# Low halves of the split gate and up weights: a subtraction on VectorE, or an adding transfer issued by GpSimd

## The chip, the cores and the metric

The kernel runs on one core of one Trainium2 chip. The metric is the device time of one execution in microseconds (us). Before the change the median of three executions is 1720.19 us (1717.99 to 1720.61). Trace times below count from the start of the span of one profiled execution, which itself took 1718.67 us.

## What is computed

One decoder layer on 576 tokens (512 of a prompt, 64 of eight short sequences) with model width 1024. It has three parts: a gated feed-forward block, a token mixer, and a second gated feed-forward block. The change touches the two feed-forward blocks:

```
def swiglu(h, w_gate, w_up, w_down):
    return (jax.nn.silu(h @ w_gate) * (h @ w_up)) @ w_down

h = modulate(rms_norm(x, n1_g), sh1, sc1)
x = x + 0.5 * g1 * swiglu(h, w1_gate, w1_up, w1_down)
```

`w_gate` and `w_up` are 1024 x 2816 in float32, `w_down` is 2816 x 1024. Everything is float32.

## The kernel before, in words

**High and low halves.** TensorE multiplies in a rounded format (float32r). To keep float32 accuracy every operand is split in two: `hi` is the rounded copy, `lo` is the source minus `hi`. A product is then three matmuls: hi x hi, hi x lo, lo x hi (`prod`, lines 675 to 683: for each of four chunks `wh*xh`, `wh*xl`, `wl*xh`, so 12 matmuls of 128x288 and the third of them is the first that reads the weight's `lo`). The split of a weight tile is made by `put_hi` (line 692, ScalarE writes `hi`) and `put_lo` (line 700, VectorE subtracts, line 707).

**Pairs.** The hidden width is cut into 22 blocks of 128 columns. Blocks 0 and 1 are computed plainly (`Plain`); each block from 2 on is a `Pair`: its gate and up columns are taken together as a 2x2 block product with seven products instead of eight (`p1` to `p7`). The weights of a pair come as two raw tiles `p` and `q` (float32, 128x1024 each, in `wraw`). From them four split tiles are made, each holding `hi` and `lo`, in the buffer ring `whl`:

- a: blocks a11 and a22, from `p` (128x1024), read by products p1 and p4
- b: block a12, from half of `q` (128x512), read by p2
- s: sums s3 and s1, from the tile `sum` that step `S` writes (line 818), read by p5 and p7
- u: sums s2 and s4, from the same tile `sum` after the steps `U` and `V` have overwritten its two halves (lines 829 and 832), read by p6 and p3

There is one tile `sum`, and in the feed-forward blocks the ring `whl` has four buffers. A buffer is free once the last product that reads it has ended.

**Order of the work.** For pair i the function `ffn` (line 928) emits: the splits of pair i (`splits`, line 840), p1(i), p2(i), the end of the pair before, p4(i-1), then p5(i), p6(i), p3(i), p7(i). After blocks 4, 10, 15 and 21 (`GROUPS`) the down projection of the group follows, 16 rows of matmuls at line 522; in the first three of these it stands between p6 and p3. A scheduler turns this into one fixed order per engine; it uses its own estimate of durations and may move instructions of one engine past each other where their data allow. On the chip each engine then runs its list strictly in order.

Pair 2 of each block is split step by step in a hand-written order (`BEGIN`, `INTO_FFN2`) by `put_hi` and `put_lo`; pairs 3 to 21 go through `splits`. So `splits` runs 19 times per feed-forward block, 38 times in all. The end of a pair on VectorE and ScalarE: line 892 multiplies p4's result in, lines 720 and 723 split the gated result.

GpSimd has little to do in these blocks: line 509, one small add for each down projection row. All loads are issued by SyncE (SP): raw weights at line 713, down weights at line 130.

Of the kernel before, what the change touches and what calls it, by code (L numbers as in the profile page):

```python
# [10 lines left out]
AF = mybir.ActivationFunctionType  # L11
ALU = mybir.AluOpType
# [63 lines left out]
def layer_kernel(ctx: ExitStack, tc: tile.TileContext, a):  # L76
    nc = tc.nc
    PE, DVE, ACT, POOL = nc.tensor, nc.vector, nc.scalar, nc.gpsimd
# [36 lines left out]
    def weight(tag, shape, dt, bufs):  # L115
        turn[tag] += 1
        own = now[tag] is not None and turn[tag] % (bufs + 1) == 0
        return (now[tag] if own else wp).tile(
            [P] + shape, dt, tag=tag, name=nm(tag), bufs=1 if own else bufs
        )  # L120
# [4 lines left out]
    def whl(shape):  # L125
        return weight("whl", shape, F32R, 4)
# [121 lines left out]
    for i in range(2):  # L248
        for n in range(NT):
            rows = P if n < 4 else NS  # L250
            t = first.tile([rows, 512], F32, name=nm("xt"))
            src = a["x_prompt"][0, n * P:(n + 1) * P] if n < 4 else a["x_sample"].rearrange("b l d -> (b l) d")
# [436 lines left out]
        return t  # L689

    class Weights:
        def put_hi(self, names, src, neg=False):
            hl = whl([2, len(names), 512])
            if neg:
                ACT.activation(out=hl[:, 0], in_=src, func=AF.Copy, scale=-1.0)
            else:
                ACT.copy(out=hl[:, 0], in_=src)  # L697
            self.hl[names] = hl, src, neg
# [96 lines left out]
    class Pair(Weights):  # L795
# [42 lines left out]
            self.put_lo(("s2", "s4"))  # L838

        def splits(self):  # L840
            for f in (self.ah, self.al, self.bh, self.bl, self.S, self.Sh, self.Sl, self.U, self.V, self.Uh, self.Ul):
                f()

        def p1(self):
            self.A = bank()
# [141 lines left out]
    for i in range(2):  # L987
        for n in range(NT):
            m = P if n < 4 else NS
            ACT.activation(  # L990
                out=junk[0:m, i], in_=xtok[n, i], func=AF.Square, accum_out=ss[0:m, i, n:n + 1]
# [54 lines left out]
    for c in range(KC):  # L1046
# [5 lines left out]
        out=t5, in0=r5, scalar=-0.5 / D, in1=r5, op0=ALU.mult, op1=ALU.mult)  # L1052
    steps["r51"] = lambda: DVE.scalar_tensor_tensor(
        out=t5, in0=s5, scalar=D * EPS, in1=t5, op0=ALU.add, op1=ALU.mult)
# [3 lines left out]
        out=xall[:, :, NP:T], in_=psS[:, 0:KC * NS].rearrange("p (c t) -> p c t", c=KC))  # L1058
# [432 lines left out]
    for n in range(NT):  # L1491
        m = P if n < 4 else NS
# [7 lines left out]
        out=rs.bitcast(I32), in0=t5.bitcast(I32), scalar1=-1.0, scalar2=float(0x5F3759DF), op0=ALU.mult, op1=ALU.add  # L1500
# [7 lines left out]
    for g in range(8):  # L1508
        DVE.tensor_tensor(
            out=wd8[:, g, :].rearrange("p (b l) -> p b l", l=LS),  # L1510
# [326 lines left out]
```

## Time and profile before

| what | value |
|---|---|
| median of 3 executions | 1720.19 us |
| the profiled execution, its own time | 1718.67 us |
| its span (first to last instruction) | 1716.6 us |
| TensorE (PE) busy | 1683.7 us, 98% |
| VectorE (DVE) busy | 1049.4 us, 61% |
| ScalarE (ACT) busy | 686.6 us, 40% |
| GpSimd (POOL) busy | 209.0 us, 12% |
| first feed-forward block's matmuls | about 36 to 452 us |
| second feed-forward block's matmuls | about 1310 to 1707 us |

How to read the rows that follow: in a timeline row stand the start, the duration, the engine, the line of the kernel, the operation, the tiles (output <- input), the count, and in brackets how long the engine had stood idle and what ended that. `whl<-sum` is a split of an s or u tile, `whl<-wraw` of an a or b tile; `xs` and `xa` are the split activations. PE is the matmul, PEld the weight load, SPq a transfer issued by SyncE. A `PE ... x12` row is one product. In the table of waits a row reads: engine and line that waited, `<-` what it waited for, total us, how often, the longest. In a table of windows, `PEclk` is the granted TensorE clock as a share of full speed.

### The profile page before, as it was taken

The page shows a single profiled execution, that of the slowest core. Times are in us where ns is not written, and L with a number is a line of the kernel's source. Part 1 is how long each engine was busy: PE and PEld are TensorE (multiplying, and loading weights), DVE is VectorE, ACT ScalarE, POOL GpSimd, SP SyncE. Part 2 cuts the span into 40 slices and gives each one's busy share as a digit, 9 for nine tenths or more (in the row PEclk, how much of TensorE's full clock was granted, in tenths as well). Part 3 has the DMA queues.
Part 4 walks back from the last instruction along what each step waited for, and adds up shares of the span by engine and source line. Part 5 has one row for each costly group of instructions (what it writes and reads, how often), then busy time and mean ns, then how long its engine had stood idle before and what let it go on. Part 6 is the DMA issues. An engine that isn't in the chain of part 4 may idle for free.

```text
span 1716.6 us, 30444 instructions
## 1 busy us (share of the span) xinstructions
PE 1683.7 (98%) x12588; PEld 1610.9 (94%) x12588; DVE 1049.4 (61%) x1758; ACT 686.6 (40%) x1137; POOL 209.0 (12%) x263
## 2 busy tenths in 40 slices
PE   7999999999999999999999999999999999999997
PEld 4879999999999999999999889999999999999997
DVE  6856847676765745745745546422547958666773
ACT  5533524335534333333333333322235525344354
POOL 0000000000421302302202101220021000000002
PEclk9999999999999999999999999999999999999999
DMA  9443444323454433444424335342330323323231
GB/s 301 132 145 98 134 139 129 99 87 95 146 163 140 142 115 125 132 123 125 149 83 143 100 115 161 103 154 75 99 103 21 87 80 92 99 84 89 86 99 56
DMA packets 279773, 199.52 MB, mean 116 GB/s; under 512 B 9801, under 2 KB 253769, under 8 KB 279634
## 3 DMA queue, kind: packets, MB, share of 16 engines
q1 hardware_dynamic: 279634, 197.58, 38.4%
q8 instruction: 98, 1.61, 0.4%
q14 instruction: 41, 0.34, 0.1%
HBM read 183.12 MB, written 14.42 MB: 115 GB/s over the span
## 4 chain that ended last, share of the span: by engine, by line
PE 88%; DVE 4%; DMA 4%; ACT 2%; issue 1%; SPq 0%; POOL 0%; POOLq 0%; DVEq 0%; ACTq 0%
PE ps L522 47%; PE ps L679 24%; PE ps L1236 5%; PE ps L1452 3%; PE ps L265 2%; DMA wraw<-in_w_down_dram 1%; DMA ada<-in_w_ada_dram 1%; DVE whl L707 1%; PE ps L1366 1%; PE ps L1244 1%; PE ps L1328 1%; DMA xa<-in_w_ada_dram 1%; ACT whl L697 1%; PE ps L1372 1%; PE ps L1344 0%
## 5 line engine op out<-in xcount | busy, mean ns | idle before, releaser
L522 PE MATMUL ps<-xa,whl 128*128 128x288 f32 x2784 | 378.4, 295 | 0.5 <-DVE whl L142 0.3
L522 PEld LDWEIGHTS ps<-xa,whl 128*128 128x128 f32 x2784 | 370.9, 188 | 7.6 <-issue 3.4
L679 PE MATMUL ps<-xa,whl 128*128 128x288 f32 x2064 | 292.8, 296 | 1.9 <-ACT whl L697 1.0
L679 PEld LDWEIGHTS ps<-xa,whl 128*128 128x128 f32 x2064 | 279.1, 188 | 10.5 <-issue 2.5
L142 DVE TENSOR_TENSOR whl<-wraw,whl 128x1024 fp32r<-128x1024 f32 x100 | 126.2, 1270 | 212.4 <-ACT whl L141 208.4
L522 PE MATMUL ps<-c,wd 128*128 128x288 f32 x1824 | 246.7, 295 | 0.0
L522 PEld LDWEIGHTS ps<-c,wd 128*128 128x128 f32 x1824 | 243.2, 188 | 2.6 <-issue 1.7
L679 PE MATMUL ps<-xs,whl 128*128 128x288 f32 x1680 | 239.7, 296 | 1.6 <-ACT sn L688 1.4
L679 PEld LDWEIGHTS ps<-xs,whl 128*128 128x128 f32 x1680 | 228.5, 188 | 7.5 <-ACT sn L688 4.9
L522 PE MATMUL ps<-c,whl 128*128 128x288 f32 x1368 | 194.9, 298 | 0.0
L522 PEld LDWEIGHTS ps<-c,whl 128*128 128x128 f32 x1368 | 184.1, 188 | 2.7 <-DVE S L1391 0.8
L141 ACT CAST whl<-wraw 128x1024 fp32r<-128x1024 f32 x100 | 104.0, 1046 | 107.3 <-PE ps L522 47.6
L509 POOL TENSOR_TENSOR x<-x,s 128x64 f32<-128x64 f32 x72 | 34.4, 478 | 909.4 <-DVE s L508 909.2
L503 DVE SCALAR_TENSOR_TENSOR x<-ps,gate,x 128x288 f32<-128x288 f32 (+1 forms) x128 | 61.5, 483 | 135.3 <-PE ps L522 134.9
L697 ACT CAST whl<-sum 128x1024 fp32r<-128x1024 f32 x80 | 84.0, 1050 | 86.3 <-DVE sum L832 58.2
L707 DVE TENSOR_TENSOR whl<-sum,whl 128x1024 fp32r<-128x1024 f32 x80 | 98.0, 1225 | 30.2 <-ACT whl L697 28.2
L697 ACT CAST whl<-wraw 128x1024 fp32r<-128x1024 f32 (+1 forms) x84 | 70.6, 841 | 98.5 <-PE ps L679 84.8
L1236 PEld LDWEIGHTS ps<-whl,xa 128*128 128x128 f32 x768 | 94.1, 194 | 5.1 <-DVE whl L142 3.4
L1236 PE MATMUL ps<-whl,xa 128*128 128x256 f32 x768 | 95.6, 286 | 3.2 <-DVE whl L142 3.2
L909 ACT CAST wd<-wraw 128x640 fp32r<-128x640 f32 (+2 forms) x58 | 45.3, 782 | 123.6 <-PE ps L522 116.7
L707 DVE TENSOR_TENSOR whl<-wraw,whl 128x1024 fp32r<-128x1024 f32 (+1 forms) x84 | 81.2, 967 | 9.5 <-ACT whl L697 9.1
L688 ACT COPY sn<-ps 128x288 f32<-128x288 f32 x126 | 50.1, 398 | 59.2 <-PE ps L679 57.7
(264 smaller groups left out, 1835.2 us busy)
## 6 DMA issues: line engine op xcount, KB each, us to landing
wraw<-in_w_in_dram SPq DMA_DIRECT2D x80, 512.0 KB
ada<-in_w_ada_dram SPq DMA_DIRECT2D x56, 512.0 KB
wraw<-in_w_gate_dram SPq DMA_DIRECT2D x88, 256.0 KB
wraw<-in_w_up_dram SPq DMA_DIRECT2D x88, 256.0 KB
wraw<-in_w_down_dram SPq DMA_DIRECT2D x32, 384.0 KB
wraw<-in_w_down_dram SPq DMA_DIRECT2D x32, 320.0 KB
S<-in_state_ret_dram SPq DMA_DIRECT2D x32, 256.0 KB
wraw<-in_w_b_dram SPq DMA_DIRECT2D x16, 512.0 KB
```

The source lines that it names most:

```text
L141: ACT.copy(out=hi, in_=raw)
L142: (eng or DVE).tensor_tensor(out=lo, in0=raw, in1=hi.bitcast(F32), op=ALU.subtract)
L503: DVE.scalar_tensor_tensor(out=x[:, o:o + w], in0=ps[:, :w], scalar=g[:, c, 0:1], in1=x[:, o:o + w], op0=ALU.mult, op1=ALU.add)
L509: return lambda: POOL.tensor_tensor(out=x[:, NP:T], in0=x[:, NP:T], in1=u, op=ALU.add)
L522: PE.matmul(ps[:, :H], lhsT=s[:, k, c0:c0 + P], rhs=m[:, HALF[h]], start=k == 0 and z == 0, stop=k == kc - 1 and z == 2,)
L679: PE.matmul(ps[:, :H], lhsT=s[:, j * P:(j + 1) * P], rhs=m[:, j, :], start=fresh and j == 0 and z == 0, stop=j == 3 and z == 2, skip_group ...
L688: ACT.copy(out=t, in_=ps[:, :H])
L697: ACT.copy(out=hl[:, 0], in_=src)
L707: DVE.tensor_tensor(out=hl[:, 1], in0=src, in1=hl[:, 0].bitcast(F32), op=ALU.subtract)
L909: ACT.copy(out=hl[:, 0], in_=self.raw[c])
L1236: PE.matmul(ps[:, :DV], lhsT=s, rhs=m, start=i == 0, stop=i == 23)
L1452: PE.matmul(ps, lhsT=s, rhs=m[:, kx % 2, :], start=kx == 0 and z == 0, stop=kx == KC - 1 and z == len(terms) - 1,)
```

## The change

From pair 3 on the split is made by a new function `put`. ScalarE writes `hi` as before; a second ScalarE operation writes the negated rounded copy into the `lo` place; then GpSimd issues a transfer that adds the source into it, so that `lo = -hi + source`. The subtraction on VectorE (line 707) is gone for these tiles. The order of steps is written into `splits`.

```
+        def put(self, names, src):
+            hl = whl([2, len(names), 512])
+            ACT.copy(out=hl[:, 0], in_=src)
+            ACT.activation(out=hl[:, 1], in_=src, func=AF.Copy, scale=-1.0)
+            POOL.dma_start(out=hl[:, 1], in_=src, accum_op=ALU.add)
+            for i, m in enumerate(names):
+                self.w[m] = (hl[:, 0, i], hl[:, 1, i])
...
         def splits(self):
-            for f in (self.ah, self.al, self.bh, self.bl, self.S, self.Sh, self.Sl, self.U, self.V, self.Uh, self.Ul):
-                f()
+            self.put(("a11", "a22"), self.p)
+            self.put(("a12",), self.q[:, 0:1])
+            self.S()
+            self.put(("s3", "s1"), self.sum)
+            self.U()
+            self.V()
+            self.put(("s2", "s4"), self.sum)
```

In the changed kernel lines behind this point stand 9 to 14 higher; `put`'s three operations are its lines 695, 696 and 697.

**PE, one pair in the first feed-forward block.** Before; whl_1997 is the pair's s tile, whl_2002 its u tile, whl_2125 and whl_2128 are a and b of the next pair, whl_1989 is a of this one:

```order
L679 MATMUL ps_2061<-xa_367,whl_1997 128x288 x12
L679 MATMUL ps_2005<-xa_495,whl_2002 128x288 x12
L679 MATMUL ps_2061<-xs_79_466,whl_2002 128x288 x12
L679 MATMUL ps_2005<-xs_83_499,whl_1997 128x288 x12
L679 MATMUL ps_2141<-xa_363,whl_2125 128x288 x12
L679 MATMUL ps_2156<-xs_78_463,whl_2128 128x288 x12
L679 MATMUL ps_2005<-xa_502,whl_1989 128x288 x12
```

The same place in the changed kernel; s is whl_2023, u whl_2029, the next pair's a and b are whl_2153 and whl_2157, a of this pair is whl_2013:

```order
L679 MATMUL ps_2089<-xa_367,whl_2023 128x288 x12
L679 MATMUL ps_2033<-xa_495,whl_2029 128x288 x2
L679 MATMUL ps_2089<-xs_79_466,whl_2029 128x288 x2
L679 MATMUL ps_2173<-xa_363,whl_2153 128x288 x2
L679 MATMUL ps_2033<-xa_495,whl_2029 128x288 x10
L679 MATMUL ps_2089<-xs_79_466,whl_2029 128x288 x10
L679 MATMUL ps_2033<-xs_83_499,whl_2023 128x288 x12
L679 MATMUL ps_2173<-xa_363,whl_2153 128x288 x10
L679 MATMUL ps_2188<-xs_78_463,whl_2157 128x288 x2
L679 MATMUL ps_2033<-xa_502,whl_2013 128x288 x6
L679 MATMUL ps_2188<-xs_78_463,whl_2157 128x288 x10
L679 MATMUL ps_2033<-xa_502,whl_2013 128x288 x6
```

The order of the products is the same (p5, p6, p3, p7, then p1 and p2 of the next pair and p4 of this one). Moved forward are the first two matmuls of some products, those that read no weight `lo`; the ten that follow stand behind the wait for `lo`.

**VectorE, the same step of a pair.** Before, from s's subtraction to u's; then p4's result (line 892), a's subtraction of the next pair, and the split of the gated result (line 723):

```order
L707 TENSOR_TENSOR whl_2133<-sum_2131,whl_2133 128x1024
L829 TENSOR_TENSOR sum_2131<-sum_2131,wraw_2119 128x512
L832 TENSOR_TENSOR sum_2131<-sum_2131,wraw_2120 128x512
L858 TENSOR_TENSOR g_2169<-ps_2156,sn_2154 128x288
L707 TENSOR_TENSOR whl_2138<-sum_2131,whl_2138 128x1024
L892 TENSOR_TENSOR g_2033<-ps_2005,g_2033 128x288
L707 TENSOR_TENSOR whl_2258<-wraw_2252,whl_2258 128x1024
L723 TENSOR_TENSOR c_2186<-g_2033,c_2185 128x576
```

In the changed kernel (line 872 is 858 of before, 906 is 892, 838 is 829, 732 is 723, 841 is 832):

```order
L872 TENSOR_TENSOR g_2201<-ps_2188,sn_2186 128x288
L906 TENSOR_TENSOR g_2061<-ps_2033,g_2061 128x288
L838 TENSOR_TENSOR sum_2161<-sum_2161,wraw_2147 128x512
L732 TENSOR_TENSOR c_2218<-g_2061,c_2217 128x576
L841 TENSOR_TENSOR sum_2161<-sum_2161,wraw_2148 128x512
```

The subtractions are gone; `U` (838) now stands behind the multiplication with p4's result (906), and `V` (841) behind the split of the gated result (732).

**GpSimd.** Where it had only line 509's adds, it now has four transfers for each pair, in the order a, b, s, u:

```order
L697 DMA whl_2013<-wraw_2007 128x1024
L697 DMA whl_2017<-wraw_2008 128x512
L697 DMA whl_2023<-sum_2021 128x1024
L697 DMA whl_2029<-sum_2021 128x1024
L697 DMA whl_2153<-wraw_2147 128x1024
```

Each of them waits for the ScalarE operation that wrote the negated copy; `U` in turn has to wait until s's transfer has read `sum`.

## The prediction

> **What bounds the kernel now.** I read the page's head first, then the waits, then the timeline of one pair.
>
> ```profile
> span 1716.6 us, 30444 instructions
> PE 1683.7 (98%) x12588; PEld 1610.9 (94%) x12588; DVE 1049.4 (61%) x1758; ACT 686.6 (40%) x1137; POOL 209.0 (12%) x263
> ```
>
> TensorE is busy 98% of the span, so what the change takes off VectorE can win at most some 30 us; what it lays on TensorE's way counts in full. The question is how much time there is between a free weight buffer and the product that needs its contents. The waits say what the splits wait for:
>
> ```profile
> ACT whl L697 <- PE ps L679: 112.9, 73, 10.3
> ACT whl L697 <- DVE sum L832: 58.2, 36, 3.2
> PE ps L679 <- DVE whl L707: 0.4, 1, 0.4
> ```
>
> ScalarE's `hi` copies wait 73 times for a product to end, that is for a buffer, and 36 times for `V`; TensorE waits for a `lo` once, 0.4 us. One pair in full, second feed-forward block:
>
> ```profile
> 1440.92 1.76 PE L679 MATMUL ps<-xs,whl 128*128 128x288 f32 x12
> 1442.52 1.75 PE L679 MATMUL ps<-xa,whl 128*128 128x288 f32 x12
> 1442.77 0.62 ACT L697 CAST whl<-wraw 128x512 fp32r<-128x512 f32 x1 [1.25 <-PE ps L679]
> 1444.11 3.36 PE L679 MATMUL ps<-xs,whl 128*128 128x288 f32 x24
> 1444.31 1.05 ACT L697 CAST whl<-sum 128x1024 fp32r<-128x1024 f32 x1 [0.58 <-PE ps L679]
> 1445.39 1.23 DVE L707 TENSOR_TENSOR whl<-sum,whl 128x1024 fp32r<-128x1024 f32 x1
> 1446.66 0.69 DVE L829 TENSOR_TENSOR sum<-sum,wraw 128x512 f32<-128x512 f32 x1
> 1447.31 4.95 PE L679 MATMUL ps<-xa,whl 128*128 128x288 f32 x36
> 1447.38 0.69 DVE L832 TENSOR_TENSOR sum<-sum,wraw 128x512 f32<-128x512 f32 x1
> 1448.18 1.05 ACT L697 CAST whl<-sum 128x1024 fp32r<-128x1024 f32 x1 [1.87 <-DVE sum L832]
> 1449.27 1.23 DVE L707 TENSOR_TENSOR whl<-sum,whl 128x1024 fp32r<-128x1024 f32 x1 [0.82 <-ACT whl L697]
> 1449.48 1.04 ACT L697 CAST whl<-wraw 128x1024 fp32r<-128x1024 f32 x1
> 1450.99 0.68 ACT L720 CAST c<-g 128x576 fp32r<-128x576 f32 x1
> 1451.91 0.75 DVE L723 TENSOR_TENSOR c<-g,c 128x576 fp32r<-128x576 f32 x1
> 1452.10 0.56 PE L679 MATMUL ps<-xs,whl 128*128 128x288 f32 x3
> ```
>
> The PE rows are p3, p7, p1 and p2, then p4, p5 and p6, then the next p3: 12 matmuls in 1442.52 - 1440.92 = 1.60 us, a period of 1452.10 - 1440.92 = 11.18 us. When p7 ends (1444.11) s's buffer is free, and at 1444.31 ScalarE begins s; subtraction, `U`, `V`, u's copy and u's subtraction follow, done at 1450.50. p6, which reads u, starts at 1447.31 + 2 x 1.60 = 1450.51. So this chain, free buffer to u's `lo`, is 6.39 us long, beside 6.40 us of other products: no slack but the 0.27 us of p6's first two matmuls. And it closes on itself: p6, p3, p7 free the buffer for the next s.
>
> **The change part by part.** *VectorE and ScalarE.* Per pair VectorE loses these subtractions:
>
> ```profile
> L707 DVE TENSOR_TENSOR whl<-sum,whl 128x1024 fp32r<-128x1024 f32 x80 | 98.0, 1225 | 30.2 <-ACT whl L697 28.2
> L707 DVE TENSOR_TENSOR whl<-wraw,whl 128x1024 fp32r<-128x1024 f32 x44 | 53.6, 1218 | 4.6 <-ACT whl L697 4.2 <-issue 0.3
> L707 DVE TENSOR_TENSOR whl<-wraw,whl 128x512 fp32r<-128x512 f32 x40 | 27.6, 690 | 5.0 <-ACT whl L697 4.8
> ```
>
> That is 2 x 1.225 + 1.218 + 0.690 = 4.36 us, 166 us over 38 pairs. ScalarE gains as many negated copies, priced like the copies above: 2 x 1.05 + 1.04 + 0.62 = 3.76 us a pair. In this stage:
>
> ```profile
> 1431.00:1442.00 11.00, 11.00 (x85) 11.00 (x85) 9.40 (x14) 6.13 (x10) 0.00 (x0) 1.00 0.34 97
> ```
>
> The columns are PE, PEld, DVE, ACT, POOL, clock, share and rate of the transfers. ScalarE goes from 6.13 to some 9.9 us in 11, so it doesn't become the bound; VectorE from 9.4 to 5, which wins nothing, since TensorE hardly waited for it.
>
> *The adding transfer.* The trace has none. Call X the time from the end of the negated copy to the landing. Its nearest rows are plain loads: one of 36 KB and one of 384 KB.
>
> ```profile
> 1.18 0.39 SPq L225 DMA_DIRECT2D ada<-in_c_dram  x1
> 3.63 1.05 ACT L257 ACTIVATE ada<-ada 9x1024 f32<-9x1024 f32 x1 [1.61 <-DMA ada<-in_c_dram]
> ada<-in_c_dram SPq DMA_DIRECT2D x1, 36.0 KB
> ...
> 1458.59 1.11 SPq L130 DMA_DIRECT2D wraw<-in_w_down_dram  x2
> 1462.04 0.83 ACT L909 CAST wd<-wraw 128x768 fp32r<-128x768 f32 x1 [0.34 <-DMA wraw<-in_w_down_dram]
> wraw<-in_w_down_dram SPq DMA_DIRECT2D x32, 384.0 KB
> ```
>
> From issue to use they took 2.45 and 3.45 us, so 1.00 us for 348 KB more, 2.87 ns per KB. By that line 512 KB moved once take 2.45 + 476 x 0.00287 = 3.82 us. An addition has to fetch the source and the old contents: 1024 KB, 2.45 + 988 x 0.00287 = 5.29 us. Beside raw loads, which hold the transfer engines for 0.34 of the time, the moving part stretches by 1/0.66: 2.45 + 2.84/0.66 = 6.75 us. I take X = 5.3 us: two reads, no crowding, since GpSimd's issuing, which no row prices, could go either way. The ends are 2.45 and 6.75 us.
>
> The Trainium skill (DMA: Bandwidth & Descriptors, "Anatomy of one DMA — SWDGE (gpsimd) path") fits a transfer issued by GpSimd as 2.0 us plus its bytes at 436 GB/s; for 512 KB that gives an estimate of 3.2 us, and the sum below would come to some 1900 us by it. The trace's 384 KB row, 3.45 us, is above that page's line (2.9 us).
>
> *The chain with it.* Count from the landing of u, when p6's last ten matmuls start. p6 and p3 ten each and p7 twelve: 32 x 1.60/12 = 4.27. To s's copy 0.20 (1444.11 to 1444.31), copy and negated copy 2 x 1.05: 6.57. Then X. `U` 0.1 later, 0.69 long; now the gated split (0.75, line 723) stands between `U` and `V`, `V` 0.69, and 0.11 to u's copy (1447.38 + 0.69 to 1448.18): 6.57 + X + 2.34 = 8.91 + X. Copy and negated copy of u: 11.01 + X. X again, and the next u has landed: a period of 11.01 + 2X, against 11.18. `U` really needs s's transfer to be over, since it overwrites what that reads. The loss per pair is 2X - 0.17 = 10.4 us.
>
> b is not on this chain: its buffer frees after p3, 1.6 us before s's, and its transfer is half as big; p2 waits for it, in time that would be spent waiting for s anyway. a has the period to itself. GpSimd's four transfers are in order behind line 509's adds only at a group's end, where b waits for p3 in any case.
>
> *Cover.* In the group ends the order puts some 44 down projection matmuls (38 in the last) between p5's last ten matmuls and p6's, where u is waited for:
>
> ```profile
> 1375.88 31.69 PE ps L522 x239
> ```
>
> 0.133 us each, 5 to 6 us hidden, 4 times per block: 8 x 5.5 = 44 us off. And the modulation matmuls strewn into the first block fall into waits:
>
> ```profile
> L265 PE MATMUL ps<-ada,cs 128*32 128x512 f32 x224 | 32.9, 605 | 3.5 <-DMA ada<-in_w_ada_dram 3.5
> ```
>
> 14 strips, 6 of them in that block, 14 us; I take 10 off.
>
> *The clock.* TensorE will now stand still for X less a's copy and two matmuls (1.05 + 0.27), some 4 us, before each p6. The start of the kernel shows what a gap does:
>
> ```profile
> 28.84 0.66 PE L277 MATMUL ps<-ident,ada 128*128 128x128 f32 x4 [1.92 <-ACT ada L271]
> ...
> 24.00:28.00 4.00, 2.51 (x20) 1.00 1.18 304
> 28.00:32.00 4.00, 2.88 (x10) 0.68 1.00 320
> 32.00:34.00 2.00, 2.00 (x9) 0.78 1.03 304
> 34.00:36.00 2.00, 2.00 (x7) 1.00 1.16 303
> ```
>
> After a 1.92 us gap the granted clock was 0.68 and then 0.78, over these 6 us 0.71 on average, and full again from 34 us on. At 0.71 the 4.27 us stretch behind the gap takes 6.0 us, 1.7 more. I take half of that, 0.85 us a pair, because the row is a single case with other matmuls: 32 us.
>
> The Trainium skill (TensorE: Matmul & The Clock Gate, "Part 1: The HAM clock gate (the "warmup" mystery)") has the clock halve after an idle window of about 3.4 us and return after as much busy time. By it nearly every pair would lose 1.7 us, and the sum would be an estimated 2124 us. The trace agrees in kind, but its clock fell after a shorter gap.
>
> *Sum.* 38 x 10.4 = 395; less 44, less 10, plus 32: 373 us. On the profiled execution's own 1718.67 us that gives 2092 us; the median of before, 1720.19, is 1.5 us higher, which doesn't matter here.
>
> **The rivals.**
>
> *A quick transfer.* If the old contents cost no second pass and GpSimd's issue is short, X = 3.1, halfway from the smallest load to one pass: loss 6.03, 38 x 6.03 - 44 - 10 = 175, 1894 us, without a clock loss, the gaps (3.1 - 1.32 us) being shorter than the 1.92 us above. For it: both sides lie in SBUF. Against it: the sum of two operands needs both. Chance 0.2.
>
> *A slow one.* Issue on GpSimd and the addition add up to X = 8: loss 15.8, 38 x 15.8 - 44 - 10 + 32 = 578, 2297 us. For it: no row shows GpSimd's issue, and four transfers per pair meet the raw loads. Chance 0.15.
>
> *The clock stays down.* With bursts of some 4 us between gaps, the clock is half throughout: 4.27 us a pair in place of 0.85, 38 x 3.42 = 130 more, 2222 us. For it the 0.68 row; against it that the clock came back within about 5 us of steady work. Chance 0.13.
>
> *Not slower.* If s's copy did not have to wait for p7, the whole chain could run a pair ahead, and TensorE would wait for nothing new: 1718 us, as before. It decides at one place, the wait of s's copy for a buffer; or X would have to be under 0.1 us. Against it: the row at 1444.31 shows that wait, four buffers are all in use, and in the changed order s's transfer still stands directly before u's, with one `sum`. Chance 0.03.
>
> **How the numbers follow.** The forecast, X near 5.3 with some clock loss, has 0.49. Range: the low end is the quick rival's 1894; the high end takes X = 6.75 (loss 13.3) and the whole clock loss of 4.27: 38 x 17.6 - 44 - 10 = 615, 2334. That holds the clock rival and X up to about 8.5, and leaves out a quick transfer under 3.1 us (0.1), a slower one (0.07) and the last rival (0.03). A measurement of this kernel tells 0.2%, 3.4 us, from no change. Only the last rival lies within that or below: 0.02 same, 0.01 faster; slower 0.97.
>
> **What would show it.** Right: p6's third matmul waits for a transfer in nearly every pair, `U` waits for s's transfer, the period is about 21 to 22 us, TensorE's busy share falls to about 80%, subtractions on L707 remain only for pairs 0 to 2. X is read from the end of the negated copy (line 696) to the start of `U` (line 838) in the changed profile. Wrong: periods near 11 us, or waits on b's transfer longer than on u's; if the gaps are as forecast and the time is longer, the matmuls between them are slower, and the clock is the cause.

## The result and the profile after

The changed kernel takes 2104.76 us (median of 4 runs, 2098.83 to 2107.44), the kernel before 1720.4 us: a ratio of 1.2232, 95% interval 1.2203 to 1.2261. It is slower by 384 us, and the predicted 2092 us was 12.8 us short. The profiled execution took 2105.39 us.

The head of the page, with the row of the granted clock in 40 slices:

```profile
span 2103.6 us, 31094 instructions
...
PE 1822.5 (87%) x12588; PEld 1699.2 (81%) x12588; DVE 897.8 (43%) x1606; ACT 814.6 (39%) x1289; POOL 339.3 (16%) x415
...
PEclk9999779799789999999999999999989889879889
```

TensorE runs the same 12588 matmuls, and is busy for 139 us longer with them: the clock row falls to 7 and 8 in the slices of the two feed-forward blocks, and nowhere in the middle. VectorE is relieved (1049.4 to 897.8 us), and nothing gains by it. The waits that took the place of those shown of before:

```profile
PE ps L679 <- DMA whl<-sum: 146.1, 67, 4.3
ACT whl L695 <- PE ps L679: 115.7, 49, 10.3
...
PE ps L679 <- DMA whl<-wraw: 34.6, 39, 2.9
...
DVE sum L838 <- DMA whl<-sum: 30.4, 33, 2.9
```

TensorE, which waited 0.4 us for a `lo`, now waits 67 times for the transfer of s or u, up to 4.3 us. ScalarE's copies (line 695 now) still wait for a product to free a buffer, and `U` (line 838) waits for s's transfer. One pair of the second block, in the order in which the loop runs:

```profile
1702.00 1.76 PE L679 MATMUL ps<-xs,whl 128*128 128x288 f32 x12
1702.20 1.05 ACT L695 CAST whl<-sum 128x1024 fp32r<-128x1024 f32 x1 [0.40 <-PE ps L679]
...
1703.16 1.05 ACT L696 ACTIVATE whl<-sum 128x1024 fp32r<-128x1024 f32 x1
...
1704.50 0.86 POOL L697 DMA_DIRECT2D whl<-sum  x1 [1.88 <-ACT sn L688]
1705.10 1.61 PE L679 MATMUL ps<-xs,whl 128*128 128x288 f32 x10 [0.54 <-DMA whl<-wraw]
...
1709.04 0.69 DVE L838 TENSOR_TENSOR sum<-sum,wraw 128x512 f32<-128x512 f32 x1 [1.04 <-DMA whl<-sum]
...
1709.65 0.75 DVE L732 TENSOR_TENSOR c<-g,c 128x576 fp32r<-128x576 f32 x1
1710.32 0.69 DVE L841 TENSOR_TENSOR sum<-sum,wraw 128x512 f32<-128x512 f32 x1
...
1711.08 1.04 ACT L695 CAST whl<-sum 128x1024 fp32r<-128x1024 f32 x1
1712.03 1.05 ACT L696 ACTIVATE whl<-sum 128x1024 fp32r<-128x1024 f32 x1
...
1713.38 0.86 POOL L697 DMA_DIRECT2D whl<-sum  x1 [8.02 <-ACT whl L696]
...
1718.48 2.77 PE L679 MATMUL ps<-xa,whl 128*128 128x288 f32 x10 [3.56 <-DMA whl<-sum]
...
1721.05 1.62 PE L679 MATMUL ps<-xs,whl 128*128 128x288 f32 x10
...
1722.51 1.75 PE L679 MATMUL ps<-xa,whl 128*128 128x288 f32 x12
...
1724.30 1.05 ACT L695 CAST whl<-sum 128x1024 fp32r<-128x1024 f32 x1
```

Read it as a loop. p7 has freed a buffer, and s is copied and negated (to 1704.21). Its transfer is issued at 1704.50, and `U` starts at 1709.04, 4.83 us after the negated copy. The gated split (732) stands between `U` and `V`; u's copies end at 1713.08; p6's last ten matmuls start at 1718.48, 5.40 us later. These ten take 2.77 us where ten after a short wait (1705.10) take 1.61. 5.82 us after the landing the next s copy starts.

The same reading for the 24 pairs that have no group end in or next to them gives these means in us, worked out row by row from the timeline. "Landing to s copy" is p6, p3 and p7; X is counted from the end of the negated copy to the first instruction that had waited for the transfer.

| | landing to s copy | s's two copies | X of s | `U` to u copy | u's two copies | X of u | period |
|---|---|---|---|---|---|---|---|
| predicted | 4.47 + 0.85 | 2.10 | 5.3 | 2.24 | 2.10 | 5.3 | 22.5 |
| changed kernel | 6.68 | 2.01 | 5.05 | 2.08 | 2.00 | 5.58 | 23.4 |

(The predicted period has 0.1 us between s's landing and `U`, which the measured X includes.)

A second table uses one instruction per pair as a mark, VectorE's product of the halves (line 887 before, 901 after). From mark to mark, an ordinary pair took 11.99 us before on average and 23.49 after (32 of them; half of those of before took 11.2 or less). The six pairs with a group end inside a block took 45.70 and 49.69. So 32 x 11.50 = 368 us were lost in ordinary pairs and 6 x 3.99 = 24 at group ends; some 6 us came back at the end of the program. That is the 387 us by which the spans differ.

### The profile page after: what moved, and what is told of

It reads as the page before. It is cut to its first block, busy times and chain, and to the rows that moved or that the text cites. A ratio compares the mean times of both kernels' runs of the same rounds, so it can differ in the third digit from the quotient of the medians.

```text
span 2103.6 us, 31094 instructions
## 1 busy us (share of the span) xinstructions
PE 1822.5 (87%) x12588; PEld 1699.2 (81%) x12588; DVE 897.8 (43%) x1606; ACT 814.6 (39%) x1289; POOL 339.3 (16%) x415
## 3 DMA queue, kind: packets, MB, share of 16 engines
q0 software_dynamic: 21888, 69.74, 18.0%
q8 instruction: 98, 1.61, 0.3%
## 5 line engine op out<-in xcount | busy, mean ns | idle before, releaser
L679 PE MATMUL ps<-xa,whl 128*128 128x288 f32 x2064 | 377.8, 332 | 203.0 <-DMA whl<-sum 146.1
L679 PEld LDWEIGHTS ps<-xa,whl 128*128 128x128 f32 x2064 | 328.7, 216 | 247.5 <-DMA whl<-sum 171.4
L522 PE MATMUL ps<-xa,whl 128*128 128x288 f32 x2784 | 378.4, 296 | 0.5 <-DVE whl L142 0.3
L522 PEld LDWEIGHTS ps<-xa,whl 128*128 128x128 f32 x2784 | 370.9, 188 | 7.6 <-issue 3.4
L679 PE MATMUL ps<-xs,whl 128*128 128x288 f32 x1680 | 293.8, 328 | 46.4 <-DMA whl<-wraw 33.2
L679 PEld LDWEIGHTS ps<-xs,whl 128*128 128x128 f32 x1680 | 269.6, 217 | 62.0 <-DMA whl<-wraw 42.8
L522 PE MATMUL ps<-c,wd 128*128 128x288 f32 x1824 | 252.6, 298 | 1.6 <-ACT c L729 1.3
L141 ACT CAST whl<-wraw 128x1024 fp32r<-128x1024 f32 x100 | 104.0, 1046 | 107.4 <-PE ps L522 47.6
L697 POOL DMA_DIRECT2D whl<-wraw x76 | 65.7, 865 | 441.3 <-ACT whl L696 400.5
L827 DVE TENSOR_TENSOR sum<-wraw,wraw 128x1024 f32<-128x1024 f32 x40 | 49.1, 1227 | 188.6 <-issue 150.1
L697 POOL DMA_DIRECT2D whl<-sum x76 | 65.6, 863 | 379.5 <-ACT whl L696 303.2
L695 ACT CAST whl<-wraw 128x1024 fp32r<-128x1024 f32 x76 | 62.8, 827 | 115.0 <-PE ps L679 110.6
L872 DVE TENSOR_TENSOR g<-ps,sn 128x288 f32<-128x288 f32 x40 | 18.3, 457 | 151.1 <-PE ps L679 151.1
```

What stands on the lines that cost most here:

```text
L141: ACT.copy(out=hi, in_=raw)
L522: PE.matmul(ps[:, :H], lhsT=s[:, k, c0:c0 + P], rhs=m[:, HALF[h]], start=k == 0 and z == 0, stop=k == kc - 1 and z == 2,)
L679: PE.matmul(ps[:, :H], lhsT=s[:, j * P:(j + 1) * P], rhs=m[:, j, :], start=fresh and j == 0 and z == 0, stop=j == 3 and z == 2, skip_group ...
L697: POOL.dma_start(out=hl[:, 1], in_=src, accum_op=ALU.add)
L827: DVE.tensor_tensor(out=self.sum, in0=self.q[:, 1:2].broadcast_to([P, 2, 512]), in1=self.p, op=ALU.add)
L872: DVE.tensor_tensor(out=g, in0=self.C[:, :H], in1=self.s1, op=ALU.subtract)
```

## The experiments

Four theories were to be told apart. Theory 1, the prediction's: a loop with two transfers of some 5 us in series. Theory 2: the transfers' throughput, or their crowd on GpSimd's queue. Theory 3: ScalarE's added copies. The clock theory adds to the first that matmuls behind a long gap run slow. Ratios are against the kernel before on the same chip (1719.03 to 1720.58 us).

| run | median us | ratio, 95% interval | ordinary pair, us | group end, us |
|---|---|---|---|---|
| e1_vector_add | 1764.44 | 1.0256 [1.0240, 1.0272] | 13.33 | 46.02 |
| e2_no_addition | 1994.83 | 1.1609 [1.1572, 1.1646] | 20.61 | 47.02 |
| e3_uv_apart | 1966.54 | 1.1438 [1.1402, 1.1475] | 18.68 | 51.88 |
| e4_a_and_b_only | 1800.53 | 1.0470 [1.0451, 1.0489] | 13.57 | 50.71 |
| e5_s_and_u_only | 2056.54 | 1.1960 [1.1942, 1.1978] | 22.34 | 48.00 |
| e6_fill | 2106.39 | 1.2250 [1.2230, 1.2270] | 22.31 | 56.16 |
| e7_lo_last | 2010.72 | 1.1691 [1.1668, 1.1714] | 20.49 | 49.59 |
| e8_apart_lo_last | 1906.42 | 1.1097 [1.1072, 1.1121] | 16.51 | 52.83 |
| e9_fill_between | 2081.03 | 1.2087 [1.2063, 1.2111] | 22.26 | 51.31 |
| e10_halves | 2040.27 | 1.1862 [1.1842, 1.1881] | 21.32 | 50.24 |
| e11_before_lo_last | 1715.29 | 0.9968 [0.9957, 0.9980] | 11.87 | 45.31 |
| e12_a_only | 1749.68 | 1.0169 [1.0155, 1.0183] | 12.42 | 48.28 |

**The transfer, replaced by VectorE.**

```diff
-            POOL.dma_start(out=hl[:, 1], in_=src, accum_op=ALU.add)
+            DVE.tensor_tensor(out=hl[:, 1], in0=src, in1=hl[:, 1].bitcast(F32), op=ALU.add)
```

> The negated copies stay, but VectorE adds the source to them (one TENSOR_TENSOR of 1.23 us for 128x1024) where the transfer did. Nothing is left out. Theory 1 (two transfers in series in the loop s copy, s transfer, U, V, u copy, u transfer, p6, p3, p7): the period falls from 11.01 + 2X to about 11.01 + 2 x 1.23 = 13.5 us, less what the group ends hide: 1750 to 1805 us, with no wait on a transfer left. Theory 3 (ScalarE's added copies, 3.76 us a pair, carry the loss): not much below 2000 us. Of the 384 us lost, theory 1 gives the added copies no more than 2 x 1.05 x 38 = 80 us.

1764.44 us. The group of p6 and its like, which after `|` has the idle time before it, waits for nothing here:

```profile
L679 PE MATMUL ps<-xa,whl 128*128 128x288 f32 x2064 | 307.5, 299 | 0.8 <-ACT whl L695 0.3 <-DVE h L897 0.2
```

In the changed kernel the same group idles 203.0 us and takes 332 ns for a matmul, not 299:

```profile
L679 PE MATMUL ps<-xa,whl 128*128 128x288 f32 x2064 | 377.8, 332 | 203.0 <-DMA whl<-sum 146.1 <-ACT whl L695 54.6 <-DMA whl<-wraw 1.4
```

Theory 3 falls: the negated copies, with an addition at the place of the subtraction, cost 44 us. The other 340 come in with the transfers.

**The transfer without its addition.**

```diff
-            POOL.dma_start(out=hl[:, 1], in_=src, accum_op=ALU.add)
+            POOL.dma_start(out=hl[:, 1], in_=src)
```

> The transfer stays on GpSimd's queue with the same source, shape and place, but overwrites the negated copy and does not add; left out is the addition, so the low part is the source itself. If the second read costs what the prediction took for it (1.47 us for 512 KB), X falls from 5.1 and 5.6 us to 3.6 to 4.1 us, twice a pair: 38 x 2.9 = 112 us off, about 1995 us. If the price lies in the issue and the landing on GpSimd's queue and the addition is nearly free, X stays within 0.3 us and the time at 2080 to 2105 us.

1994.83 us, 110 less, as the second read asks. Over the 24 pairs X fell from a mean of 5.05 to 3.45 us (s) and from 5.58 to 4.29 us (u). What the transfer queue and GpSimd's group show, without the addition:

```profile
L697 POOL DMA_DIRECT2D whl<-sum x76 | 40.1, 528 | 349.3 <-ACT whl L696 263.8 <-ACT sn L688 78.8 <-DMA wraw<-in_w_up_dram 6.7
```

```profile
q0 software_dynamic: 21888, 69.74, 10.1%
```

and with it, in the changed kernel:

```profile
L697 POOL DMA_DIRECT2D whl<-sum x76 | 65.6, 863 | 379.5 <-ACT whl L696 303.2 <-ACT sn L688 68.3 <-DMA wraw<-in_w_up_dram 8.0
```

```profile
q0 software_dynamic: 21888, 69.74, 18.0%
```

The same 21888 packets and 69.74 MB. The last figure is their time as a share of the 16 engines' span: 0.101 x 1994.3 = 201 us without the addition, 0.180 x 2103.6 = 379 us with it, 1.88 times as much. The issue takes 0.86 us of GpSimd in place of 0.53. So the addition costs 1.3 to 1.6 us on 512 KB, near the 1.47 that the prediction took for a second pass; up to 0.33 us of it can be GpSimd's longer issue, which was not tried apart. The two X fell by 2.9 us together and an ordinary pair by as much (23.49 to 20.61): both transfers stand in the loop with their whole length.

**`U` and `V` apart from s's transfer.**

```diff
-            self.U()
-            self.V()
-            self.put(("s2", "s4"), self.sum)
+            DVE.tensor_tensor(out=self.q[:, 1], in0=self.sum[:, 1], in1=self.p[:, 0], op=ALU.add)
+            DVE.tensor_tensor(out=self.q[:, 0], in0=self.q[:, 1], in1=self.q[:, 0], op=ALU.add)
+            self.put(("s4", "s2"), self.q)
```

> U and V are written into the pair's raw tile q in place of the tile that s's transfer reads, so U no longer waits for s's transfer to land; the same four transfers, the same bytes, the same queue. Nothing is left out. Theory 1 (two transfers in series): u's copies follow s's at once, U and V (with the split between them, 2.1 us) overlap s's transfer of 5.1 us, so the period falls by 3 to 5 us of 23.3: 1915 to 1990 us. Theory 2 (the transfers' throughput or the crowd of them on GpSimd's queue sets the pace): both transfers now overlap, each gets slower by as much, and the time stays at 2080 to 2105 us.

1966.54 us: 138 less with all four transfers and all their bytes in place. So the pace of the changed kernel was not set by what the transfers can move, which is theory 2: ordinary pairs with the same transfers in them follow each other 4.8 us sooner. What the edit takes out is the wait of `U` for s's transfer. From the end of s's negated copy to u's copy there were 7.1 us in the changed kernel (X of s, and `U` to u copy); here there are 3.6, on average over the same 24 pairs. The two transfers themselves still stand one behind the other:

```profile
1720.60 0.86 POOL L697 DMA_DIRECT2D whl<-sum  x1 [1.53 <-ACT whl L696]
...
1722.57 1.59 PE L679 MATMUL ps<-xs,whl 128*128 128x288 f32 x10 [1.27 <-DMA whl<-wraw]
...
1724.24 1.05 ACT L695 CAST whl<-wraw 128x1024 fp32r<-128x1024 f32 x1 [3.58 <-PE ps L679]
...
1726.36 1.59 PE L679 MATMUL ps<-xa,whl 128*128 128x288 f32 x10 [0.49 <-DMA whl<-sum]
...
1726.54 0.86 POOL L697 DMA_DIRECT2D whl<-wraw  x1 [5.09 <-ACT whl L696]
```

s's transfer, issued at 1720.60, has landed by 1726.36, when p5's last ten matmuls start; u's is issued at 1726.54. Over the 24 pairs u's issue comes 0.7 us after s's landing on average, and X is 5.3 us for s and 5.4 for u, much as before. What the transfers of s and u would cost each other if they overlapped was not tried. A part of the gain went into new waits, both for b's transfer. `V` (line 855 here), which overwrites b's source, waits for it:

```profile
L855 DVE TENSOR_TENSOR wraw<-wraw x38: 691/692/695, 81.8 to 1898.4; 128x512 f32<-128x512 f32 x38
its engine sat idle before it (us, times) until:
  DMA whl<-wraw: 108.5, 38
```

That is 2.9 us in each of the 38 pairs. In 36 of them a product ends last before u's copy, as in the rows above: p2, whose last ten matmuls start at 1722.57 with b's landing, ends at 1724.16, and at 1724.24 ScalarE begins u's copy.

**Only a and b, and only a.** In both, the groups that don't go by transfer get back their copy and subtraction as before.

```diff
             self.put(("a11", "a22"), self.p)
             self.put(("a12",), self.q[:, 0:1])
-            self.S()
-            self.put(("s3", "s1"), self.sum)
-            self.U()
-            self.V()
-            self.put(("s2", "s4"), self.sum)
+            for f in (self.S, self.Sh, self.Sl, self.U, self.V, self.Uh, self.Ul):
+                f()
```

> a and b go by transfer as in the changed kernel, s and u by VectorE's subtraction as before: 768 of the 1792 KB per pair are left to transfers. Nothing is left out. Theory 1: the loop through s and u is free of transfers and gets only a delay where a's and b's low parts come late and a's negated copy holds ScalarE up: 1720 to 1800 us. Theory 2 (bytes or number of transfers): half the transfers and 0.43 of the bytes keep 0.43 to 0.5 of the loss: 1885 to 1915 us. The prediction priced a and b at nothing, so by its own sum 1720 us.

```diff
             self.put(("a11", "a22"), self.p)
-            self.put(("a12",), self.q[:, 0:1])
-            self.S()
...
-            self.put(("s2", "s4"), self.sum)
+            for f in (self.bh, self.bl, self.S, self.Sh, self.Sl, self.U, self.V, self.Uh, self.Ul):
+                f()
```

> Only a goes by transfer, b, s and u by VectorE's subtraction. Nothing is left out. The prediction priced a at nothing because it has the period to itself: 1720 us. The trace with a and b shows p1 waiting some 1.2 us for a in part of the pairs, because ScalarE makes a's two copies behind u's and the transfer takes 4.9 us more: by that up to 38 x 1.2 = 46 us, 1740 to 1765 us.

1800.53 and 1749.68 us. With s and u on VectorE, a costs 29 us and b another 51, where the prediction had nothing. How a comes late, in the run with a alone:

```profile
1457.44 1.05 ACT L706 CAST whl<-sum 128x1024 fp32r<-128x1024 f32 x1 [1.24 <-PE ps L679]
...
1458.99 1.06 ACT L695 CAST whl<-wraw 128x1024 fp32r<-128x1024 f32 x1 [0.15 <-PE ps L679]
...
1459.95 1.05 ACT L696 ACTIVATE whl<-wraw 128x1024 fp32r<-128x1024 f32 x1
...
1461.30 0.85 POOL L697 DMA_DIRECT2D whl<-wraw  x1 [11.50 <-ACT whl L696]
...
1465.20 0.43 PE L679 MATMUL ps<-xs,whl 128*128 128x288 f32 x2
...
1465.88 3.19 PE L679 MATMUL ps<-xs,whl 128*128 128x288 f32 x22 [0.25 <-DMA whl<-wraw]
```

a's copies can only start behind u's (1457.44 to 1458.49). From there to p1's third matmul, which would start at 1465.63 (1465.20 + 0.43), are 7.1 us. a takes 7.4: 0.5 until its copy starts, 2.0 for both copies, 0.3 to the issue and 4.6 of transfer. So p1, whose last ten matmuls open the group of 22, waits, here 0.25 us and at most 2.3; TensorE's waits for a's transfer come to 19.5 us in all, and with b by transfer too those for a and b come to 54.2. a has not "the period to itself", but what is left of it behind u's copy.

**Only s and u.**

```diff
-            self.put(("a11", "a22"), self.p)
-            self.put(("a12",), self.q[:, 0:1])
-            self.S()
+            for f in (self.ah, self.al, self.bh, self.bl, self.S):
+                f()
             self.put(("s3", "s1"), self.sum)
```

> s and u go by transfer as in the changed kernel, a and b by VectorE's subtraction as before. Nothing is left out. It is the mirror of the run with a and b alone, which cost 80 us over before. Prediction (a and b lie beside the loop and are priced at nothing): 2080 to 2105 us. If the parts' costs add up (each transfer costs its own share wherever it stands): 2105 - 80 = 2025 us, and less still if the crowd of transfers matters.

2056.54 us, 48 below the changed kernel: between the two expectations. Beside s and u, a and b together cost 48 us, by themselves 80. The timeline shows where 21 us of the 48 come from:

```profile
1671.84 0.76 DVE L732 TENSOR_TENSOR c<-g,c 128x576 fp32r<-128x576 f32 x1 [0.74 <-ACT c L729]
1674.05 0.69 DVE L838 TENSOR_TENSOR sum<-sum,wraw 128x512 f32<-128x512 f32 x1 [1.46 <-DMA whl<-sum]
...
1674.78 0.69 DVE L841 TENSOR_TENSOR sum<-sum,wraw 128x512 f32<-128x512 f32 x1
```

The gated split (732) is over here before `U` can start; in the changed kernel it stands between `U` and `V`. p2, and p4 behind it, no longer wait for b's transfer (1705.10 in the pair above), so p4's result and its split come earlier. `U` to u's copy fell from 2.08 to 1.53 us, 38 x 0.55 = 21 us. Landing to s copy fell by 0.41 us; why is open.

**Matmuls in the gap.** After p6's second matmul:

```diff
...
+                if fill and j == 0 and z == 1:
+                    jk, mms = bank(), [mm]
+                    for n in range(24):
+                        mms.append(PE.matmul(
+                            jk[:, :H], lhsT=wh[:, n % 4 * P:(n % 4 + 1) * P], rhs=xh[:, n % 4, :],
+                            start=n == 0, stop=n == 23, skip_group_check=True,
+                        ))
+                    in_order(mms)
+                    after = mms[-1]
...
-            prod(self.A, self.w["s2"], op("T2"), False)
+            prod(self.A, self.w["s2"], op("T2"), False, self.f > 2)
```

> 24 more matmuls (u's hi weights, a spare PSUM bank, 3.2 us at full clock; their result isn't used) stand after p6's second matmul, in the time in which TensorE waits for u's transfer, some 3.6 us. The output is that of the changed kernel. Clock theory: without the gap the granted clock stays up, and the stretch from u's landing to the next s copy, 6.7 us in the changed kernel, shrinks to 4.5 to 5.2 us: 2020 to 2050 us, mean clock above 0.96. If the slow matmuls behind the gap come from something else (the transfers' traffic, say): no gain, 2105 us or up to 40 us more where the 24 don't fit.

2106.39 us, no gain, though the mean granted clock rose from 0.922 to 0.967. The table shows why: an ordinary pair gained 1.2 us, and a group end, whose gap is already filled by down projection matmuls, lost 6.5. The second version leaves them out there:

```diff
-            prod(self.A, self.w["s2"], op("T2"), False, self.f > 2)
+            prod(self.A, self.w["s2"], op("T2"), False, self.f > 2 and self.f not in (5, 11, 16))
```

> The 24 unused matmuls again, in the gap before u's landing, but left out of the pairs 5, 11 and 16, in which a group's down projection already fills that gap; in the first run with them these pairs lost 39 us and the 32 others won 38. The output is that of the changed kernel. Clock theory: 2105 - 38 = 2067 us, within 10. If the 38 us were chance between runs, 2100 to 2110.

2081.03 us: 24 of the 38 us, so there is a gain, and the expectation missed by 14 us, of which 10 stand at the group ends (51.31 against 49.69 in the changed kernel), for a reason that stays open. Landing to s copy fell from 6.68 to 4.98 us on average (median 6.84 to 4.56; full clock gives 4.47), with the same transfers around it. The mean granted clock rose from 0.922 to 0.968. So the matmuls behind the gap were slow from the clock, not from the traffic. The fill doesn't win all of that in the period. It meets the gap in two ways, both to be seen in e6_fill, where the extra matmuls are line 690 and the products line 680:

```profile
1698.54 5.64 PE L690 MATMUL ps<-xa,whl 128*128 128x288 f32 x24
...
1704.55 1.56 PE L680 MATMUL ps<-xa,whl 128*128 128x288 f32 x10
...
1719.42 3.35 PE L690 MATMUL ps<-xa,whl 128*128 128x288 f32 x24
...
1725.06 1.59 PE L680 MATMUL ps<-xa,whl 128*128 128x288 f32 x10 [1.76 <-DMA whl<-sum]
```

Where the clock had already fallen, the 24 take 5.64 us and last beyond u's landing; else they take 3.35 us, and a wait of 1.76 us is left.

**The low parts last.** Inside a product, in the changed kernel:

```diff
-        for j in range(4):
-            for z, (s, m) in enumerate(((wh, xh), (wh, xl), (wl, xh))):
+        for z, (s, m) in enumerate(((wh, xh), (wh, xl), (wl, xh))):
+            for j in range(4):
```

> Inside a product the order of the 12 matmuls is changed: the four that read the low part of the weights come last, not third, sixth, ninth and twelfth. Nothing is left out; transfers as in the changed kernel. Loop theory: eight matmuls of p6 and eight of p3, not two and two, can run ahead of u's landing, 20 of 32 remain behind it: at least 12 x 0.133 = 1.6 us a pair off, up to 2.5 with the lowered clock: 1995 to 2045 us. If throughput of the transfers sets the pace: 2105 us.

2010.72 us, 94 less. Landing to s copy fell from 6.68 to 3.79 us, 2.9 us: 1.6 for the 12 matmuls that now run ahead, the rest, worked out and not tried by itself, because fewer run at the lowered clock. `U` to u copy fell too, from 2.08 to 1.50 us, and X of u rose by 0.4. Together with `U` and `V` apart:

> U and V apart (1966.5 us) and the low parts last together. Nothing is left out. If both act on the one loop, the gains add up: 1966 less 38 x 1.6 to 2.5 = 1870 to 1905 us, still slower than before by 150 us or more, since one transfer of 5 us and four added copies stay in the loop. If a floor of the transfers (GpSimd's issue, four a pair) sets in, no lower than about 1930.

1906.42 us, 1.4 above the range expected. Together they gain 198 us and not 138 + 94 = 232; a floor near 1930 doesn't show, and where the 34 us went was not tried.

**Half transfers.**

```diff
-            POOL.dma_start(out=hl[:, 1], in_=src, accum_op=ALU.add)
             for i, m in enumerate(names):
+                POOL.dma_start(out=hl[:, 1, i], in_=src[:, i], accum_op=ALU.add)
```

> Each 512 KB transfer is issued as two of 256 KB, one for each of the two operands that it makes; b stays one. Nothing is left out. In the changed kernel b's 256 KB took 3.6 us from the end of the negated copy, the 512 KB of s 4.85. If products and U wait for the half they need, each step of the loop falls by up to 1.2 us: 38 x 2 x 1.2 = 91 off, less what the group ends hide: 2020 to 2050 us. If GpSimd's issuing (0.86 us each, now seven a pair) or a wait for both halves sets in, each step grows by up to 0.86 us: 2105 to 2170 us.

2040.27 us, 64 less, in the range of the first case.

```profile
1621.71 1.75 POOL L698 DMA_DIRECT2D whl<-sum  x2 [1.94 <-ACT sn L688]
...
1625.11 0.68 DVE L838 TENSOR_TENSOR sum<-sum,wraw 128x512 f32<-128x512 f32 x1
...
1626.65 0.69 DVE L841 TENSOR_TENSOR sum<-sum,wraw 128x512 f32<-128x512 f32 x1 [0.86 <-DVE sum L838]
1626.70 1.57 PE L679 MATMUL ps<-xa,whl 128*128 128x288 f32 x10 [1.75 <-DMA whl<-sum]
```

`U` starts 3.4 us after the first half's issue, not 4.54 as in the changed kernel. X fell by 0.80 us for s and 0.92 for u on average, and at best it was 3.62 us for the 256 KB, against 4.82 for 512: 1.2 us for the second 256 KB and 2.4 that are fixed, where the prediction's line had 1.47 and 2.35 (2.45 less 36 KB).

**The kernel before with the low parts last.** The same two lines as in e7_lo_last, in the kernel before.

> The kernel before, without any transfer, with the low parts last inside each product. Nothing is left out. Its loop of copies and subtractions gets 1.6 us of slack a pair, but TensorE waits there for nothing but some microseconds: 1710 to 1720 us, a gain of 10 us at most.

1715.29 us, 5.3 us below the kernel before, ratio 0.9968 (0.9957 to 0.9980): the only version that beats both, and it has no transfer.

## Why the prediction was right, and which terms were off

**The loop** was read rightly: its steps, their order and the two waits that the text named are in the timeline, and e2_no_addition shows that both transfers stand in it with their whole length, since an ordinary pair fell by as much as the two X together. e3_uv_apart shows the price of one of the two waits, that of `U`: 3.5 us a pair.

**X** was taken at 5.3 us and measured at 5.05 for s and 5.58 for u; the smallest of the 48 is 4.82. That an addition costs about a second read is borne out by e2_no_addition, where it fell by 1.60 and 1.29 us against 1.47 in the prediction. Why u's is larger is open: a's transfer is issued 1.9 us behind it, but in e5_s_and_u_only, where a has none, X of u was 5.53 us all the same. Raw loads meet it in both runs, and their part was not tried. Its largest was 9.41 us. The Trainium skill (DMA: Bandwidth & Descriptors, "Anatomy of one DMA — SWDGE (gpsimd) path") gives the estimate of 3.2 us that the prediction weighed; the median X of s without the addition was 3.21 us, so the page's line fits the plain copy here. With the addition the median was 4.85 us.

**The rivals.** The quick transfer (X = 3.1) exists only without the addition, and there not without a clock loss: landing to s copy stayed at 6.5 us; X = 8 came up only in single pairs. "Not slower" falls with the loop. "The clock stays down" is refuted in size: landing to s copy never exceeded 7.29 us in the 24 pairs, and at half clock it would be 8.74.

**The clock term was the step that was mis-sized.** The prediction halved the one case it had, to 0.85 us a pair; landing to s copy was 6.68 us, 2.2 more than at full clock, which is 84 us for 38 pairs and not 32. The case itself (1.7) was nearer than its half. It had also been read as the effect of one gap of 1.92 us. In the trace of before the granted clock is 0.50 from 29.46 to 32.87 us, and 1.00 on both sides of that; 0.68, 0.78 and 0.71 are averages across these edges, and in the 3.41 us before the fall TensorE was busy for 1.49 us. The Trainium skill (TensorE: Matmul & The Clock Gate, "Part 1: The HAM clock gate (the "warmup" mystery)") has the clock halve after an idle window of about 3.4 us, from which the prediction estimated 1.7 us a pair. The length agrees with the steps of 3.41 us in which the clock moves here, but TensorE was not idle in the steps after which it fell (see the end). The clock is also most of why TensorE's busy share is 87% and not the forecast 80%, since slow matmuls count as busy: it was busy for 210 us at half clock, which makes some 105 of the 139 us more.

**Cover.** The prediction took 44 us off for eight group ends. The six inside the blocks lost 4.0 us each, an ordinary pair 11.5: 45 us covered. For the modulation strips it took 10 us off; ordinary pairs lost 11.49 us in the first block, which has the strips, and 11.51 in the second: nothing was covered.

**a and b, priced at nothing,** was wrong: 48 us as they stand, 80 without s and u, by the ways that e5_s_and_u_only and e12_a_only show. The first of these ways, the split between `U` and `V`, was in the prediction's loop, but not put down to b.

**Why the sum came out near all the same.** An ordinary period was foreseen at 22.5 us and was 23.4: the clock adds 1.36, X of u 0.28, and X of s, the copies and the stretch from `U` to u's copy take off some 0.7. But the loss was counted from 11.18 us, the shortest pair before, and the ordinary pair before took 11.99 on average, which takes back 0.8 of the 0.9. So the loss of the pairs is 38 x 11.5 = 437 us where the prediction had 395 + 32 = 427, and 51 us were covered (45 and the 6 at the program's end) where it had 54: 386 against 373. That the clock's 52 us too few met errors of the other sign is luck.

## What to carry to other kernels

Before an operation is moved from an engine to a transfer, find the loop that the engine's operation closes: a transfer of 5 us costs its whole length in it, twice if a second one waits for the first. Beside the loop it costs what the time there doesn't hold (a and b: 48 of the 384 us). A busy engine's relief is worth only what others waited for it (here 0.4 us), and an operation that "has the period" has only what is left of it behind the copies that go ahead of it. Where a wait can't be avoided, let the work that doesn't need it run ahead: the order inside a product was worth 94 us in the changed kernel, and 5 us even in the one before.

## What the runs showed of the hardware

An accumulating transfer of 512 KB within SBUF, issued by GpSimd, took at best 4.82 us from the end of its producer, and 3.16 without the addition; the engines' packet time was 1.88 times as long, and GpSimd's issue 0.86 us in place of 0.53.

TensorE's clock answered to how busy TensorE was within fixed steps, not to the length of one wait. In the trace of the changed kernel the granted clock is 0.50 or 1.00 and nothing between, and it keeps either for a whole number of steps of 3.41 us. Around the pair above the steps look like this; PE's busy time stands first behind the comma, and the clock in the column before the last two:

```profile
1707.71:1711.12 3.41, 1.64 (x11) 1.36 (x10) 2.25 (x4) 1.09 (x4) 0.00 (x0) 1.00 0.26 52
1711.12:1714.53 3.41, 1.79 (x6) 1.44 (x6) 0.00 (x0) 3.41 (x5) 0.86 (x1) 0.50 0.82 239
1714.53:1717.95 3.42, 0.39 (x2) 0.04 (x1) 0.00 (x0) 0.45 (x1) 0.86 (x1) 0.50 1.09 234
1717.95:1721.36 3.41, 2.88 (x12) 2.88 (x13) 1.23 (x1) 0.07 (x1) 0.00 (x0) 0.50 0.70 136
1721.36:1724.78 3.42, 3.42 (x28) 3.42 (x28) 0.92 (x2) 2.29 (x5) 0.58 (x1) 1.00 0.00 0
```

After a step with TensorE busy for 1.64 of 3.41 us the clock fell, at 1711.12, more than 7 us before u landed; it came back at 1721.36, after a step with 2.88 us busy. Worked out for all steps of this trace from 25 us on: each of the 36 falls followed a step with TensorE busy for at most 0.52 of it, and the clock never stayed up after one below 0.46. It came back after steps of 0.84 or more, and stayed down after all of 0.81 or less. The same count in the other traces moves these bounds to 0.60 and 0.45, and to 0.83 and 0.88.

So the length of a wait is a sign, no more. In the changed kernel 104 runs of ten matmuls followed a wait: of the 67 behind waits of up to 1.64 us 66 took 1.58 to 1.61 us, and of the 37 behind waits of 1.94 to 4.33 us 31 took 2.77. But in e5_s_and_u_only, where a few matmuls stand between several short waits, 20 of the 36 behind waits of up to 1.52 us took 2.77 us too, as this one:

```profile
1660.01 2.77 PE L679 MATMUL ps<-xa,whl 128*128 128x288 f32 x10 [0.78 <-DMA whl<-sum]
```
